# A fourth seven-product pair in the down projection of the first SwiGLU of an encoder trunk

## The chip, the cores and the metric

The kernel runs on one core of one Trainium2 chip. The metric is the device time of one execution in microseconds (us); smaller is better. The engines of the core are TensorE (PE, matrix products), VectorE (DVE), ScalarE (ACT), GpSimd (POOL) and SyncE (SP, which here issues the transfers from HBM). Each works through its own instructions in the order in which the program wrote them, and they wait for one another by semaphores.

## The reference

The model is a trunk of two layers over 256 tokens of width 1024. Each layer adds half a SwiGLU, a mixer (attention) and half a SwiGLU to the residual x; all in float32. The part that the change touches is the SwiGLU ahead of the first mixer:

```python
def swiglu(h, w_gate, w_up, w_down):
    return (jax.nn.silu(h @ w_gate) * (h @ w_up)) @ w_down

    h = rms_norm(x, ffn1_norm[layer])
    x = x + 0.5 * swiglu(h, ffn1_w_gate[layer], ffn1_w_up[layer], ffn1_w_down[layer])
```

`w_gate` and `w_up` are 1024 x 2816, `w_down` is 2816 x 1024. The stages are numbered 0 (SwiGLU), 1 (even mixer), 2, 3 (SwiGLUs), 4 (odd mixer), 5 (SwiGLU).

## The kernel before

**A product.** A float32 operand is kept as two parts, a high one (a copy rounded by ACT, `high_part`) and a low one (the rest, `value - high`, by DVE, `low_part`). A product of a 128 x 128 block of activations with a 128 x 512 block of weights is three matmuls (hi·hi, hi·lo, lo·hi; `mm`, lines 474 to 476), summed in PSUM.

**Weights.** SP loads them in units of 1 MB into one of three `raw` tiles (`load`, line 382). A unit is cut into `Split`s of at most 128 x 1024, each of one or two `Piece`s 512 wide. `supply` makes the high part of the next split, and `low`, a tick later, its low part; when the last split of a unit has its low part, the next unit is loaded. The parts lie in seven places of `wp`, or, where the raw data are sums, in three places of `sum` (`shi`, `slo`). After each product `tick` runs: it adds `rate` pieces to `due`, and supplies a split if as many pieces are due as it has and a place is free (`room`). In stage 0 the rate is 0.6; from the first seven-product pair of the down on it is `DOWN_RATE`, 1.24; after the last such pair `ENDS` sets it to 0.43. Small tasks (silu, glu, transposes, sums) are generators that wait a given number of ticks between their steps. Thus the order of every engine's instructions is fixed by these counts when the program is built.

**The SwiGLU of stage 0** (`ffn`). The width 2816 is done in five chunks of 512 and one of 256 (called mixed, since its gate and up are one operand). The third chunk is itself done with fewer products (`seven_gates`). In each chunk the gate and up products of both halves of the tokens (tt = 0, 1) run, then `silu` (ACT), `glu` (DVE), and `transposed`: the result is turned over (a copy on ACT, L559; a DMA transpose, L561; another copy on ACT, L563) and split into `g_h` and `g_l`, the left operands of the down.

**The down** works through eleven pairs of 128-row blocks of `w_down` in the order of `DOWN[0]`. Pair p3 means blocks 6 and 7, done plainly: 2 blocks x 2 halves of the tokens x 2 halves of the columns are 8 products; s3 means the same by Strassen's scheme in Winograd's form, with 7 products (`seven`). A plain pair needs two splits 1024 wide. A seven-product pair needs four (`strassen`): one 512 wide (b11), then `two_sums` makes `two` on DVE (1024 wide); one 1024 wide of the raw data (b21, b22), then `other_sums` makes two sums of 512 in place in `raw` on DVE (L398); one of `two` (t7, t5) and one of the sums in place (t8, t6). It needs sums of the activations as well (`quarters`, `sums_of`): each half of the tokens is copied by ACT into a `quarters` tile (three tiles in this stage), three sums are made on DVE (lines 716 to 718), and split into `kh` and `kl` (two places). `sums_of` is asked for by `ask`: the first three positions of the order at the start of the mixed chunk, each later one three pairs ahead.

The first products of a seven-product pair go to temporary banks `M`; after the last such pair `combine` adds them to x on DVE (lines 940 to 967). The last two pairs (p10, p9) are held back, so that each quarter of the output can be finished by itself: `add_to_x` (L617) adds it to x on DVE, and a few ticks later `prepare` has PE turn x for the next stage (L530), ACT and DVE split it (`th`, L515; `tl`, L520). The next stage's first weights are `even_w_in`.

Of the kernel before, what the change touches and what calls it, by code (L numbers as in the profile page):

```python
# [33 lines left out]


DOWN = {
# [20 lines left out]
TURN_WAIT = [1, 16]  # L57
SUMS_AHEAD = {0: 3, 2: 3, 3: 3, 5: 4}
QUARTERS = {0: 3, 2: 3, 3: 3, 5: 4}
PLACES = {0: 2, 2: 2, 3: 2, 5: 3}  # L60
SUMS_WAIT = [8, 2]
SILU_WAIT = [3, 4, 2]
# [135 lines left out]
def pairs(stage):  # L198
    return [({"p": "plain", "s": "strassen"}[o[0]], int(o[1:])) for o in DOWN[stage].split()]
# [9 lines left out]
class Trunk:  # L209
# [88 lines left out]
    def plan(self):  # L298
# [56 lines left out]
        def odd():  # L355
# [4 lines left out]
            for g in range(2):  # L360
                for nh in range(2):
                    src = w_out[g * 512 : g * 512 + 512, nh * 512 : nh * 512 + 512].rearrange("(j p) n -> p j n", p=P)
                    yield [(slice(0, P), src)], 4, 512, [2], "narrow"

        yield from ffn("ffn1", 0, 0)
        yield from even()
        yield from ffn("ffn2", 0, 2)
        yield from ffn("ffn1", 1, 3)
        yield from odd()
        yield from ffn("ffn2", 1, 5)  # L370
# [291 lines left out]
    def ffn(self):  # L662
# [4 lines left out]
        down = pairs(self.now.n)  # L667
# [5 lines left out]
        def silu(tt, w, g, s):  # L673
            yield 1
            nc.scalar.activation(s[:, :w], g[:, :w], AF.Silu, scale=self.rstd_of(tt))

        def glu(tt, f0, w, u, s):
            yield 1
            m = self.t([P, 512], "glu", 3)
            nc.vector.scalar_tensor_tensor(m[:, :w], u[:, :w], self.now.r[tt], s[:, :w], op0=ALU.mult, op1=ALU.mult)  # L680
            self.spawn(transposed(tt, f0, w, m), GLU_WAIT)
# [17 lines left out]
        def quarters(tt, f, tb, at):  # L699

            block = lambda i: tb[:, (at + i) * P : (at + i + 1) * P]
            if tt == 0:
                paired[f] = self.t([P, 4, P], "quarters", QUARTERS[self.now.n])
                nc.scalar.activation(paired[f][:, 0:2, :].rearrange("p a b -> p (a b)"), tb[:, at * P : (at + 2) * P], AF.Copy)
# [5 lines left out]
        def sums_of(f):  # L710

            while f not in whole:
                yield 1
            k = paired[f]
            d = k[:, 3:4, :].to_broadcast([P, 2, P])
            nc.vector.tensor_tensor(k[:, 2:4, :], d, k[:, 2:0:-1, :], op=ALU.subtract)
            nc.vector.tensor_tensor(k[:, 1, :], k[:, 2, :], k[:, 1, :], op=ALU.subtract)
            nc.vector.tensor_tensor(k[:, 0, :], k[:, 1, :], k[:, 0, :], op=ALU.add)
            yield SUMS_WAIT[0]
            hi, lo = (self.t([P, 4, P], f"k{p}", PLACES[self.now.n], F32R) for p in "hl")  # L720
            self.high_part(hi, k)
            yield SUMS_WAIT[1]
            self.low_part(lo, k, hi)
            sums[f] = [(hi[:, i, :], lo[:, i, :]) for i in (3, 2, 1, 0)]

        K = []
        sevens = SEVEN[self.now.n]
        most = max(sevens.values())

        def x_sums():  # L730
# [19 lines left out]
            places = [(f"g0_{sum(FF_CHUNKS[:ci]) // P}_", FF_CHUNKS[ci] // P) for ci in range(max(sevens), len(FF_CHUNKS))]  # L750
            places = [(tag, n, 1) for tag, n in places[:2]] + [("k", 4, PLACES[self.now.n])] * 2
            for (tag, n, bufs), k in zip(places, (k0, k1, k2, k3)):
# [3 lines left out]
                self.low_part(lo, k, hi)  # L756
                K.append([(hi[:, q, :], lo[:, q, :]) for q in range(most)])

        def seven_gates(f0, w, pairs7):

            while len(K) < 4:
                self.tick(False)
# [9 lines left out]
            def common():  # L772

                yield 1
                while "m" not in c:
                    yield 1
                w = self.t([P, 512], "silu", SILUS[self.now.n])
                op(w, M["6"], c["m"], op=ALU.add)
                yield 1
                y = self.t([P, 512], "glu", 3)  # L780
                op(y, M["5"], w, op=ALU.subtract)
                yield 1
                nc.vector.scalar_tensor_tensor(w, M["7"], -1.0, w, op0=ALU.mult, op1=ALU.add)
                c["y"], c["w"] = y, w

            def first_gate():
                yield 1
                while "m" not in c:
                    yield 1
                s = self.t([P, 512], "silu", SILUS[self.now.n])  # L790
                op(s, M["00"], c["m"], op=ALU.add)
                yield SILU_WAIT[0]
                nc.scalar.activation(s, s, AF.Silu, scale=self.now.r[0])
                c["s"] = s
# [26 lines left out]
            def product(name, lh, piece, first, last):  # L821
                self.mm(M[name], lh, piece, first, last)
# [5 lines left out]
            for q in range(KD // 2):  # L828
# [19 lines left out]
                if last:  # L848
                    tasks.append(self.start(first_gate()))
                product("01", K[0][j], b22, q == 0, last)  # L850
                product("7", K[3][j], t7, first, last)
                product("5", K[2][j], t5, first, last)
                product("10", h[1][k], t8, q == 0, last)
                product("6", K[1][j], t6, first, last)
            self.start(common())
# [4 lines left out]
        for ci, w in enumerate(FF_CHUNKS):  # L860
            if ci in sevens:
                seven_gates(f0, w, sevens[ci])
                f0 += w // P
                continue
            self.rate = (AHEAD_RATE if ci + 1 in sevens else RATE)[self.now.n]

            tags = ["pj", "s", "s", "pj"] if ci - 1 in sevens else ["s", "s", "pj", "pj"]
            G = self.take(KD)
            S = []
            if self.now.n + ci == 0:  # L870
                both = self.first_gates(G)
            for tt in range(NT):
                g = both[tt] if self.now.n + ci == 0 else self.project(self.ready(tt), G, tags[tt])
                S.append(self.t([P, 512], "silu", SILUS[self.now.n]))
                self.start(silu(tt, w, g, S[tt]))
            U = self.take(KD)
            for tt in range(NT):
                u = self.project(self.now.hT[tt], U, tags[NT + tt])
                tasks.append(self.start(glu(tt, f0, w, u, S[tt])))
            f0 += w // P  # L880

        def ask(i):
            if i < len(down) and down[i][0] == "strassen":
                self.spawn(sums_of(2 * down[i][1]))

        w, V = FF_MIXED, self.take(KD)
        for i in range(SUMS_AHEAD[self.now.n]):
            ask(i)

        for tt in range(NT):  # L890
# [81 lines left out]
        for i, (kind, pair) in enumerate(down[:-HELD]):  # L972
            ask(i + SUMS_AHEAD[self.now.n])
            if kind == "strassen":
                seven(pair, i == order[0], i == order[-1])
                if i == order[-1]:
                    self.start(combine())
                    self.rate, self.due = ENDS[self.now.n]
                continue
            for f in (2 * pair, 2 * pair + 1):  # L980
                W[f] = self.take(2)
                for tt in range(NT):
                    for half in range(2):
                        use(f, tt, slice(half * 512, half * 512 + 512))
# [420 lines left out]
    def after(self, tt, sl, nxt):  # L1405
# [12 lines left out]
        x, gain = self.x[tt], self.last_gain  # L1418
        sq = self.t([P, 4, P], "quarters", QUARTERS[self.now.n]).rearrange("p a b -> p (a b)")
        v = self.two.tile([P, 1], F32, tag="last_v", name=self.name("v"), bufs=6)  # L1420
# [158 lines left out]
```

## Time and profile before

| | us |
|---|---|
| median of 3 runs | 935.45 |
| all runs | 935.42, 935.95, 935.45 |
| the profiled execution, its time | 935.71 |
| its span, first to last instruction | 933.7 |
| PE busy, share of the span | 99% |
| DVE busy, share of the span | 83% |
| ACT busy, share of the span | 72% |
| granted TensorE clock, mean | 0.999 |

A timeline row reads: start in us, duration in us, engine, line, operation, output <- inputs, shape, xcount of merged instructions, and in brackets how long the engine was idle before it and what ended that. PEld is TensorE's load of the stationary operand, SPq is SyncE's queue of transfers. A matmul of 512 columns is drawn 0.39 us long, but the next starts 0.23 us after it, since they are pipelined: starts, not durations, tell PE's pace. Likewise a DVE instruction of 1024 elements is drawn 1.22 us long while its successor starts 1.14 us after it.

In the profiled execution the five chunks and the mixed one of stage 0 end at 127 us, its down lasts to 186 us, and the even mixer follows.

### The profile page before, as it was taken

The numbers are of one execution on the slowest core, as the hardware profiler recorded it, in microseconds if no ns is written. First come the engines' busy times: TensorE is split into PE (matmuls) and PEld (weight loads), VectorE is DVE, ScalarE is ACT, GpSimd is POOL, SyncE is SP. The second block draws the span as 40 slices with busy tenths as digits, with TensorE's granted clock in tenths as the row PEclk, the third lists the DMA queues.
The fourth block names the chain that finished last, engine by engine and source line by source line (L and its number), as shares of the span: only waits on it lengthen the run. The fifth ranks groups of instructions, "written<-read, shape, count | busy, mean of one in ns | idle before, by whom it ended". The sixth has DMA issues, their size and how long they took to land.

```text
span 933.7 us, 12374 instructions
## 1 busy us (share of the span) xinstructions
PE 921.5 (99%) x4405; PEld 754.3 (81%) x4405; DVE 773.4 (83%) x1198; ACT 675.9 (72%) x1084; POOL 92.6 (10%) x152
## 2 busy tenths in 40 slices
PE   9999999999999999999999999999999999999997
PEld 6887888877778888888888888888878888888885
DVE  6799679778868889799878888978867696977898
ACT  7778876467777778885657879657777586778853
POOL 1300000064420000000100000008030000000001
PEclk9999999999999999999999999999999999999999
DMA  8857865644327577757466787566434367588651
GB/s 297 283 172 256 244 213 184 218 142 109 112 92 231 173 237 236 233 191 265 156 193 211 216 278 207 225 210 200 155 99 159 105 204 225 168 265 254 164 212 53
DMA packets 129341, 183.14 MB, mean 196 GB/s; under 512 B 50688, under 2 KB 63744, under 8 KB 129280
## 3 DMA queue, kind: packets, MB, share of 16 engines
q1 hardware_dynamic: 128704, 181.58, 61.8%
q8 instruction: 34, 0.56, 0.2%
q10 hardware_dynamic: 576, 0.79, 0.2%
q14 instruction: 27, 0.22, 0.1%
HBM read 169.76 MB, written 1.05 MB: 183 GB/s over the span
## 4 chain that ended last, share of the span: by engine, by line
PE 88%; DVE 7%; ACT 3%; issue 1%; POOL 0%; POOLq 0%; ACTq 0%; DVEq 0%
PE s L476 13%; PE s L475 13%; PE s L474 12%; PE pj L474 12%; PE pj L475 11%; PE pj L476 11%; DVE lo L485 3%; PE o L474 2%; PE o L476 2%; PE o L475 2%; PE o L1053 2%; PE tp L1130 1%; ACT hi L482 1%; PE tp L530 1%; PE tp L474 1%
## 5 line engine op out<-in xcount | busy, mean ns | idle before, releaser
L485 DVE TENSOR_TENSOR lo<-raw,hi 128x1024 fp32r<-128x1024 f32 (+1 forms) x372 | 377.7, 1034 | 81.8 <-ACT hi L482 80.2
L482 ACT ACTIVATE hi<-raw 128x1024 fp32r<-128x1024 f32 (+1 forms) x372 | 320.1, 892 | 53.9 <-PE s L476 12.6
L474 PE MATMUL s<-hi,th 128*128 128x512 f32 x378 | 148.1, 392 | 0.0
L475 PE MATMUL s<-lo,th 128*128 128x512 f32 x378 | 147.2, 389 | 0.2 <-DVE lo L485 0.2
L476 PE MATMUL s<-hi,tl 128*128 128x512 f32 x378 | 147.2, 390 | 0.0
L474 PE MATMUL pj<-hi,th 128*128 128x512 f32 x366 | 146.2, 399 | 0.0
L475 PE MATMUL pj<-lo,th 128*128 128x512 f32 x366 | 143.2, 391 | 0.6 <-DVE lo L485 0.4
L476 PE MATMUL pj<-hi,tl 128*128 128x512 f32 x366 | 142.8, 390 | 0.0
L475 PEld LDWEIGHTS s<-lo,th 128*128 128x128 f32 x378 | 71.0, 188 | 15.0 <-DVE lo L485 0.5
L476 PEld LDWEIGHTS s<-hi,tl 128*128 128x128 f32 x378 | 70.9, 188 | 14.9
L474 PEld LDWEIGHTS s<-hi,th 128*128 128x128 f32 x378 | 71.0, 188 | 14.5
L475 PEld LDWEIGHTS pj<-lo,th 128*128 128x128 f32 x366 | 68.9, 188 | 15.2 <-DVE lo L485 2.6
L476 PEld LDWEIGHTS pj<-hi,tl 128*128 128x128 f32 x366 | 68.7, 188 | 14.5
L474 PEld LDWEIGHTS pj<-hi,th 128*128 128x128 f32 x366 | 68.8, 188 | 14.0 <-issue 1.0
L494 POOL TENSOR_TENSOR rstd<-var,mhalf 128x1 f32<-128x1 f32 (+2 forms) x16 | 17.1, 1070 | 586.6 <-ACT th L515 309.7
L563 ACT COPY turned<-glu 128x1024 uint16<-128x1024 uint16 (+1 forms) x48 | 60.2, 1253 | 13.2 <-DMA glu<-turned 13.2
L559 ACT COPY turned<-glu 128x1024 uint16<-128x1024 uint16 (+1 forms) x48 | 46.3, 965 | 24.1 <-DVE glu L797 16.3
L482 ACT ACTIVATE shi<-raw 128x1024 fp32r<-128x1024 f32 x28 | 29.6, 1059 | 32.7 <-DVE raw L398 23.0
L474 PE MATMUL s<-hi,g_h 128*128 128x512 f32 (+1 forms) x134 | 52.5, 392 | 0.0
L476 PE MATMUL s<-hi,g_l 128*128 128x512 f32 (+1 forms) x134 | 52.0, 388 | 0.0
L475 PE MATMUL s<-lo,g_h 128*128 128x512 f32 (+1 forms) x134 | 52.0, 388 | 0.0
L482 ACT ACTIVATE shi<-two 128x1024 fp32r<-128x1024 f32 x28 | 29.6, 1058 | 23.8 <-DVE two L398 23.7
(350 smaller groups left out, 1657.3 us busy)
## 6 DMA issues: line engine op xcount, KB each, us to landing
raw<-in_ffn_w_down SPq DMA_DIRECT2D x44, 1024.0 KB, 5.1
raw<-in_ffn_w_up SPq DMA_DIRECT2D x28, 1024.0 KB, 5.1
raw<-in_ffn_w_gate SPq DMA_DIRECT2D x26, 1024.0 KB, 5.3
raw<-in_ffn_w_gate SPq DMA_DIRECT2D x35, 512.0 KB, 4.2
raw<-in_ffn_w_up SPq DMA_DIRECT2D x32, 512.0 KB, 5.2
raw<-in_odd_w_qkv SPq DMA_DIRECT2D x12, 1024.0 KB, 5.2
raw<-in_even_w_in SPq DMA_DIRECT2D x4, 1024.0 KB, 5.1
raw<-in_even_w_out SPq DMA_DIRECT2D x8, 512.0 KB, 5.7
```

The lines of the kernel that those rows point to most:

```text
L474: mm(ps, h, wh, start=first, stop=False)
L475: mm(ps, h, wl, start=False, stop=False)
L476: mm(ps, l, wh, start=False, stop=last)
L482: self.nc.scalar.activation(hi, src, AF.Copy)
L485: self.nc.vector.tensor_tensor(lo, src, hi.bitcast(F32), op=ALU.subtract)
L494: nc.gpsimd.tensor_tensor(r[:, :n], v[:, :n], self.mhalf[:, :n], op=ALU.pow)
L530: nc.tensor.transpose(tb[:, j * P : (j + 1) * P], self.x[tt][:, b * P : (b + 1) * P], self.ident)
L559: self.nc.scalar.copy(planes.rearrange("p (h c) -> p h c", h=2), back.rearrange("p (c h) -> p h c", h=2))
L563: self.nc.scalar.copy(planes.rearrange("p (c h) -> p h c", h=2), back.rearrange("p (h c) -> p h c", h=2))
L1053: self.nc.tensor.matmul(O[64 * s : 64 * s + 64, i * P : i * P + P], v(b0 + i, s, kc), pT[s][:, i, kc, :], start=(kc == 0), stop=(kc == 1),)
L1130: nc.tensor.transpose(tb[:, o : o + P], p[:, i, kc * P : kc * P + P], self.ident)
```

## The change

Pair 1 of the down of stage 0 becomes a seven-product pair, so that there are four (1, 3, 5, 7) and seven plain pairs. Its quarters come from the first chunk. The sums of the first three positions of the order, of which only pair 1 needs any, are asked for at the beginning of the fifth chunk in place of the mixed chunk's. Stages 2, 3 and 5 keep their orders and their time of asking (`None`).

```diff
 DOWN = {
-    0: "p0 p1 p2 s3 p4 s5 p6 s7 p8 p10 p9",
+    0: "p0 s1 p2 s3 p4 s5 p6 s7 p8 p10 p9",
...
+FIRST_SUMS = {0: 4, 2: None, 3: None, 5: None}
...
+        asked = 0
+
+        def ask(i):
+            if i < len(down) and down[i][0] == "strassen":
+                self.spawn(sums_of(2 * down[i][1]))
...
             self.rate = (AHEAD_RATE if ci + 1 in sevens else RATE)[self.now.n]
+            if ci == FIRST_SUMS[self.now.n]:
+                asked = SUMS_AHEAD[self.now.n]
+                for i in range(asked):
+                    ask(i)
...
-        def ask(i):
-            if i < len(down) and down[i][0] == "strassen":
-                self.spawn(sums_of(2 * down[i][1]))
-
         w, V = FF_MIXED, self.take(KD)
-        for i in range(SUMS_AHEAD[self.now.n]):
+        for i in range(asked, SUMS_AHEAD[self.now.n]):
             ask(i)
```

## The prediction

> **What bounds the kernel now.** First the head of the page, then the busy time of one stretch of the down.
>
> ```profile
> span 933.7 us, 12374 instructions
> PE 921.5 (99%) x4405; PEld 754.3 (81%) x4405; DVE 773.4 (83%) x1198; ACT 675.9 (72%) x1084; POOL 92.6 (10%) x152
> ```
>
> ```profile
> 140.00:166.00 26.00, 26.00 (x117) 21.52 (x116) 25.63 (x32) 15.44 (x20) 0.00 (x0) 1.00 0.58 205
> ```
>
> The columns of the stretch are length, PE, PEld, DVE, ACT, POOL, clock, DMA. PE is never idle in the first SwiGLU's down (127 to 186 us). But from 140 to 166 DVE is full too (25.63 of 26), and that stage is where the change puts more DVE work. The DVE rows of one period (s5 with p6 behind it) show the price of each piece, from start to start, with no wait between them:
>
> ```profile
> 142.14 0.42 DVE L716 TENSOR_TENSOR quarters<-quarters 128x256 f32<-128x256 f32 x1
> ...
> 143.13 0.42 DVE L485 TENSOR_TENSOR g_l<-turned,g_h 128x256 fp32r<-128x256 f32 x1
> 143.46 0.69 DVE L485 TENSOR_TENSOR lo<-raw,hi 128x512 fp32r<-128x512 f32 x1
> 144.06 1.22 DVE L398 TENSOR_TENSOR two<-raw 128x1024 f32<-128x1024 f32 x1
> 145.20 1.22 DVE L485 TENSOR_TENSOR lo<-raw,hi 128x1024 fp32r<-128x1024 f32 x1
> 146.34 0.68 DVE L398 TENSOR_TENSOR raw<-two,raw 128x512 f32<-128x512 f32 x1
> 147.06 0.69 DVE L398 TENSOR_TENSOR raw<-raw 128x512 f32<-128x512 f32 x1
> 147.66 1.22 DVE L485 TENSOR_TENSOR slo<-two,shi 128x1024 fp32r<-128x1024 f32 x1
> 148.80 0.42 DVE L485 TENSOR_TENSOR g_l<-turned,g_h 128x256 fp32r<-128x256 f32 x1
> 149.13 0.69 DVE L485 TENSOR_TENSOR kl<-quarters,kh 128x512 fp32r<-128x512 f32 x1
> 149.74 1.22 DVE L485 TENSOR_TENSOR slo<-raw,shi 128x1024 fp32r<-128x1024 f32 x1
> 150.87 2.35 DVE L485 TENSOR_TENSOR lo<-raw,hi 128x1024 fp32r<-128x1024 f32 x2
> ...
> 159.47 0.68 DVE L485 TENSOR_TENSOR kl<-quarters,kh 128x512 fp32r<-128x512 f32 x1
> ```
>
> So: the three sums of quarters 0.99 (142.14 to 143.13), a 512-wide low 0.60, `two` 1.14, a 1024-wide low 1.14, the two sums in place 1.32 (146.34 to 147.66), kl 0.61.
>
> Now the stage's end, as timeline rows of PE, DVE, ACT, SP and PEld:
>
> ```profile
> 127.38 0.39 PE L474 MATMUL o<-hi,g_h 128*128 128x512 f32 x1
> 168.86 0.39 PE L474 MATMUL o<-hi,g_h 128*128 128x512 f32 x1
> 161.21 4.62 DVE L485 TENSOR_TENSOR lo<-raw,hi 128x1024 fp32r<-128x1024 f32 x4
> 163.59 14.92 SPq L382 DMA_DIRECT2D raw<-in_even_w_in  x6
> 171.10 2.20 ACT L482 ACTIVATE hi<-raw 128x512 fp32r<-128x512 f32 x4 [2.36 <-DMA raw<-in_even_w_in]
> 171.77 1.29 DVE L485 TENSOR_TENSOR lo<-raw,hi 128x512 fp32r<-128x512 f32 x2 [2.06 <-ACT hi L482]
> 180.44 0.68 DVE L617 SCALAR_TENSOR_TENSOR x<-o,x 128x512 f32<-128x512 f32 x1
> 181.18 0.42 PEld L530 LDWEIGHTS tp<-mats,x 128*128 128x128 f32 x4 [0.34 <-DVE x L617]
> 184.43 0.60 PE L530 MATMUL tp<-mats,x 128*128 128x128 f32 x4
> ```
>
> This is a chain that ends exactly when PE needs it. The lows from 161.21 are p8's two, then p10's; p8's second ends at about 163.5, frees its raw tile, and SP, which waits for that, issues the mixer's first weights at 163.59. They land at 171.1 (ACT waited 2.36 for them). Their two lows stand in DVE's queue ahead of `combine` (L951 on); DVE then works without a gap from 171.77 to the end of x<-o at 181.12, and the transposes L530, which come next on PE, start at 181.18, after a wait of 0.34 for DVE's x. The matmuls of p8 on follow each other every 0.227 us, so PE was due at these transposes at 181.10. The page's chain names only PE here, since a wait of 0.1 us is all that shows: **two chains arrive together**, PE's products and DVE's lows with the load behind them.
>
> **The change, part by part.** On PE, p0 begins at 127.38 and p8 at 168.86: five plain pairs of 8 products and three of 7, 61 in 41.48 us, 0.68 us each. s1 takes one product away: **-0.68 us**, if PE ends the stage. In the Trainium skill, "TensorE: Matmul & The Clock Gate", section Back-to-back issue gap, an isolated 512-column matmul takes N/2.4 + 2.5, or 216 ns, and a sustained stream 131 ns; here three take 680, 227 each. By the page's two figures the term would be 0.65 or 0.39; the trace decides, and the sign stays.
>
> On DVE, s1 needs a 512-wide low, three 1024-wide lows, `two`, two sums in place, three sums of quarters and kl, where p1 needed two 1024-wide lows. What of it is hidden:
>
> ```profile
> 102.83 3.95 DVE L485 TENSOR_TENSOR lo<-raw,hi 128x1024 fp32r<-128x1024 f32 x3 [2.12 <-ACT hi L482]
> 118.33 1.22 DVE L485 TENSOR_TENSOR lo<-raw,hi 128x1024 fp32r<-128x1024 f32 x1
> 122.65 0.48 DVE L680 SCALAR_TENSOR_TENSOR glu<-s,rstd,silu 128x256 f32<-128x256 f32 x1 [3.10 <-ACT silu L675]
> 124.59 3.95 DVE L485 TENSOR_TENSOR lo<-raw,hi 128x1024 fp32r<-128x1024 f32 x3 [1.46 <-ACT hi L482]
> 129.56 0.69 DVE L485 TENSOR_TENSOR lo<-raw,hi 128x512 fp32r<-128x512 f32 x1 [1.02 <-ACT hi L482]
> 137.52 1.23 DVE L485 TENSOR_TENSOR slo<-raw,shi 128x1024 fp32r<-128x1024 f32 x1 [0.55 <-ACT shi L482]
> ```
>
> The quarters' sums and kl (1.60) go into the fifth chunk, into idle time such as the 2.12 before 102.83: 0. They also release the quarters tile that s7 needs, in time. The 512-wide low and `two` (1.74) stand where p1's first low stood (118.33), before an idle of 3.10: 0; without that cover 0.6. s1's second low replaces p1's second, the first of the three at 124.59: before that wp has no free place (ACT's high parts wait for PE there, as in the row of 126.22 below), so nothing more can move up. **New behind 124.59: two sums in place 1.32 and two lows 2.28, together 3.60 us.** The idle of before between there and 139 that could take it: 1.02, 0.55 and 0.45 within the row at 124.59 (3.95 less two starts of 1.14 and a duration of 1.22), 2.02. From 139.3 to 165.8 DVE has no gap. So the lateness d of p8's lows is at least 3.60 - 2.02 = 1.58 us. It is more if new gaps open, and two do, by ACT's order:
>
> ```profile
> 126.22 1.06 ACT L482 ACTIVATE hi<-raw 128x1024 fp32r<-128x1024 f32 x1 [0.30 <-PE s L476]
> 127.19 0.60 ACT L559 COPY turned<-glu 128x512 uint16<-128x512 uint16 x1
> 127.70 1.35 ACT L563 COPY turned<-glu 128x1024 uint16<-128x1024 uint16 x1
> 129.44 0.62 ACT L482 ACTIVATE g_h<-turned 128x512 fp32r<-128x512 f32 x1
> 129.96 0.46 ACT L675 ACTIVATE silu<-s,rstd 128x256 f32<-128x256 f32 x1
> 133.46 0.62 ACT L559 COPY turned<-glu 128x512 uint16<-128x512 uint16 x1 [0.97 <-DVE g_l L485]
> 133.99 1.37 ACT L563 COPY turned<-glu 128x1024 uint16<-128x1024 uint16 x1
> ```
>
> First gap: the high part of s1's last sums must wait for the sums in place (124.59 + 1.14 + 1.32, about 127.1) and takes p2's place of 126.22; behind it stand L559 (0.51), L563 (1.21), g_h (0.52), the silu (0.5). Each comes a little under 1 us later than before, the glu that needs the silu not before 130.85, while DVE is through with s1 at 129.4 and p2's lows stand behind that glu: 1.45. Second gap: at rate 0.6 the four further pieces of s1 push s3's second split from p0's fourth product to s1's first, behind L559, L563, g_h and kh. L559 waits for g_l as at 133.46, now until 134.2; then 0.53, 1.40, 0.54, 0.52 and the high part's 1.06 give 138.3, when DVE has finished `two` at 136.9: 1.4. So d = 3.60 + 1.45 + 1.4 - 2.02 = **4.4 us**; ends 1.58 (no new gap) and about 5. I take 4.4, since both gaps follow from the written order.
>
> The Trainium skill (the same page, its first table) calls ScalarE's and VectorE's queues strict FIFOs. By that the ready lows can't pass the waiting glu, and d is 4.4; if they could, it would fall towards 1.58. The trace agrees in so far as DVE sat out 3.10 us before the glu of 122.65.
>
> Does d make PE stop earlier? kl of s5 ends at 149.82 + 4.4 = 154.2, needed by s5's third product, now at 154.6; kl of s7 at 164.5 against 164.8; p8's first low at 166.8 against 168.2. All just in time: 0. At the end nothing covers it: p8's raw tile frees d later, the mixer's weights land d later (its neighbour p9 shifts alike), `combine` and x<-o end at 185.5, and PE, there at 180.42 instead of 181.10, waits 5.1 us. The gain of 0.68 is lost in that wait, and the stage ends d later. After it PE is the bound again, with no idle to give back until 200.
>
> Sum: -0.68 (PE) + 5.1 (wait) = **+4.4 us**. The profiled execution took 935.71, span 933.7, 0.26 above the median; the span should come to 938.1, the time to 935.45 + 4.4 = **939.8**. The other edits cost nothing: two copies of quarters more in the first chunk's transposes lie on ACT, which is not on the path; and s1's fifth product, the first on the bank that the last glu frees at about 131.3, comes at 135.5 (127.38 + 12 x 0.68).
>
> **Rivals.** A, as above, 939.8, own range 938.6 to 940.6. B: the order is kinder and DVE uses its idle, d 1.6: 937.0. For it: 2.02 us of gaps are there; against it: ACT's fixed order. C, the other side: PE alone ends the stage, 935.45 - 0.68 = 934.8. Its place is the transposes at 181.18; it decides if x<-o does not come later than 180.4, that is if d is below -0.7. For it: DVE's idle of 2.06 before 171.77; against it: that idle waits for a load which DVE's own lows release, so it moves with them. D: after a wait of 5.1 us PE runs slower for a while. No PE wait of this length is in this trace, so it can't tell; at half pace over the 3.25 us from these transposes to the next (184.43) it would cost that much more: 943. The Trainium skill, the same page, section on the clock gate, says the clock halves after an idle window of about 3.4 us; no run here shows it, the clock of the stretch above being 1.00.
>
> **How the numbers follow.** A 0.58, B 0.16, C 0.12, D 0.09, the rest 0.05 (a later stage gives something back, or kl stops PE too). The range leaves out C and most of D and reaches under B: 936.3 to 941.2. A measurement tells 0.2%, 1.87 us, from no change: slower A, D, a part of B and of the rest, 0.73; same C and most of B, 0.24; faster 0.03.
>
> **What would show it.** Right: x<-o of the first half some 4 us later (near 185), PEld L530 waiting about 5 us for DVE x, the first mixer load issued near 168, no PE wait before. Wrong: no wait at L530 (C), or PE waits at kl or slo in s3 to s7, which would put the price into the alternation itself.

## The result and the profile after

| | us |
|---|---|
| kernel before, median of 4 runs on the same chip | 935.7 (935.42 to 937.47) |
| changed kernel, median of 4 runs | 941.26 (940.74 to 941.88) |
| ratio, 95% interval | 1.0059 (1.0047 to 1.0071) |
| forecast, its range | 939.8 (936.3 to 941.2) |

The change makes the kernel slower by 5.6 us. The sign holds, and so does the chain that the forecast describes; the price that it put on the wait at the end of that chain does not. The size is 1.5 us over it (1.2 as a difference, 5.6 where 4.4 was forecast, since the kernel before came out at 935.7 and not at 935.45), and the median lies 0.06 us above the upper end of the range.

The head of the page of the changed kernel, its profiled execution (941.88 us):

```profile
span 940.1 us, 12375 instructions
PE 922.9 (98%) x4402; PEld 755.3 (80%) x4402; DVE 781.1 (83%) x1207; ACT 678.3 (72%) x1089; POOL 91.2 (10%) x152
```

PE is busy 1.4 us longer although it has fewer products to do, and the span grows by 6.4. PE's waits between 100 and 200 us (engine, line, what it waited for: us in total, times, longest):

```profile
PE tp L531 <- DVE x L618: 4.9, 1, 4.9
```

There is one, at the transposes, where the forecast put it. (In this kernel the lines from the sums on stand one further down than before, those of the SwiGLU's tail one to seven.) Rows of its timeline, DVE, SP, ACT and PE, in order of time:

```profile
98.69 0.42 DVE L717 TENSOR_TENSOR quarters<-quarters 128x256 f32<-128x256 f32 x1
...
104.44 0.69 DVE L486 TENSOR_TENSOR kl<-quarters,kh 128x512 fp32r<-128x512 f32 x1
...
124.56 1.23 DVE L486 TENSOR_TENSOR lo<-raw,hi 128x1024 fp32r<-128x1024 f32 x1 [1.46 <-ACT hi L483]
...
131.03 0.48 DVE L681 SCALAR_TENSOR_TENSOR glu<-s,rstd,silu 128x256 f32<-128x256 f32 x1 [1.57 <-ACT silu L676]
...
138.38 1.23 DVE L486 TENSOR_TENSOR lo<-raw,hi 128x1024 fp32r<-128x1024 f32 x1 [1.27 <-ACT hi L483]
...
163.93 0.68 DVE L486 TENSOR_TENSOR kl<-quarters,kh 128x512 fp32r<-128x512 f32 x1
165.67 4.62 DVE L486 TENSOR_TENSOR lo<-raw,hi 128x1024 fp32r<-128x1024 f32 x4
168.05 24.97 SPq L383 DMA_DIRECT2D raw<-in_even_w_in  x7
175.34 2.20 ACT L483 ACTIVATE hi<-raw 128x512 fp32r<-128x512 f32 x4 [2.05 <-DMA raw<-in_even_w_in]
176.00 1.29 DVE L486 TENSOR_TENSOR lo<-raw,hi 128x512 fp32r<-128x512 f32 x2 [1.75 <-ACT hi L483]
180.16 0.39 PE L477 MATMUL s<-hi,g_l 128*128 128x512 f32 x1
184.67 0.69 DVE L618 SCALAR_TENSOR_TENSOR x<-o,x 128x512 f32<-128x512 f32 x1
185.41 1.11 PE L531 MATMUL tp<-mats,x 128*128 128x128 f32 x4 [4.87 <-DVE x L618]
187.18 0.63 PE L477 MATMUL s<-hi,g_l 128*128 128x512 f32 x1
187.60 0.63 PE L475 MATMUL s<-hi,g_h 128*128 128x512 f32 x1
190.93 0.60 PE L531 MATMUL tp<-mats,x 128*128 128x128 f32 x4
```

The same steps as before, each 4.2 to 4.5 us later: p8's lows 161.21 to 165.67, the mixer's first load 163.59 to 168.05, its lows 171.77 to 176.00, x<-o 180.44 to 184.67. PE is through with the products at 180.39 (the start at 180.16 and 0.227) instead of 181.10, and waits.

The last three rows show what the forecast left out of its sum. Behind the wait PE's matmuls start 0.42 to 0.43 us apart (187.18, 187.60), not 0.227. From these transposes to the next it takes 190.93 - 185.41 = 5.52 us, where it took 184.43 - 181.18 = 3.25 before: **2.27 us more, after the wait has ended.** So the transposes at 190.93 are 6.50 late, 4.23 by x<-o and 2.27 by the pace. The window view of the same kernel gives the granted clock (third column from the end; the first numbers are length and PE's busy time):

```profile
140.00:166.00 26.00, 26.00 (x116) 21.52 (x116) 25.76 (x35) 16.93 (x22) 0.00 (x0) 1.00 0.50 166
...
180.55:183.47 2.92, 0.00 (x0) 0.00 (x0) 2.92 (x6) 0.00 (x0) 0.00 (x0) 1.00 0.05 4
183.48:190.30 6.82, 4.89 (x14) 4.02 (x15) 4.29 (x10) 2.48 (x8) 0.00 (x0) 0.50 0.45 152
190.31:194.00 3.69, 3.69 (x20) 3.06 (x19) 2.77 (x9) 3.34 (x8) 1.75 (x4) 1.00 0.12 7
```

The clock is halved while PE still waits, 2.9 us after its last matmul was drawn to end, and stays at half for 6.8 us, of which 190.30 - 185.41 = 4.9 fall on work. Half of those, 2.4, is about the 2.27 lost.

### The profile page after: what moved, and what is told of

The parts are those of the page before. It is cut to its first block, busy times and chain, and to the rows that moved or that the text cites. A ratio compares the mean times of both kernels' runs of the same rounds, so it can differ in the third digit from the quotient of the medians.

```text
span 940.1 us, 12375 instructions
## 1 busy us (share of the span) xinstructions
PE 922.9 (98%) x4402; PEld 755.3 (80%) x4402; DVE 781.1 (83%) x1207; ACT 678.3 (72%) x1089; POOL 91.2 (10%) x152
## 4 chain that ended last, share of the span: by engine, by line
PE 82%; DVE 10%; ACT 4%; issue 2%; DMA 1%; POOL 0%; POOLq 0%; SPq 0%; ACTq 0%; DVEq 0%
PE s L477 12%; PE s L476 12%; PE s L475 12%; PE pj L475 11%; PE pj L476 11%; PE pj L477 11%; DVE lo L486 4%; PE o L1060 2%; PE o L477 2%; PE o L475 2%; PE o L476 2%; PE tp L1137 1%; ACT hi L483 1%; DVE raw L399 1%; DVE slo L486 1%
```

## The experiments

Three questions: is the price made of x<-o's lateness alone, or also of the clock; is the lateness the sum of DVE's work and the two gaps; and is anything left of the 0.68 us of the product? Each kernel is compared with the kernel before, timed on the same chip; that one's median was 935.76 to 936.35, so differences are taken within a comparison. Line numbers shift by some lines with each edit (the transposes are L531 to L534, x<-o L618 to L621).

**PE kept at work during the wait (e1_busy).** In the changed kernel, 24 matmuls of 384 columns go into the bank of the first transposes, right ahead of them. The transposes overwrite their result, so the output is that of the changed kernel.

```diff
+        if (i, tt, half) == (1, 0, 0):
+            for _ in range(24):
+                nc.tensor.matmul(tb[:, : 3 * P], self.ident16, self.busy, start=True, stop=True)
...
+        self.busy = m16[:, 0 : 3 * P]
```

> The changed kernel with 24 idle matmuls (384 columns, result overwritten) put on PE right ahead of the transposes that wait for x, so that PE is busy in most of that wait and x comes no sooner. Theory (the wait of 4.9 us itself costs 4.2 us, and the lowered clock after it another 2): the wait for DVE x shrinks below 1 us, the matmuls behind it go at 0.227 us each instead of 0.43, granted clock of the span 0.999 instead of 0.995, and the time falls by 1.6 to 2.4 us, to 938.9 to 939.7. Rival (the pace behind the wait is slow for another reason, such as late x or late weights of the mixer): the matmuls stay at 0.43 us and the time at 941.

Measured: 940.02 us (939.64 to 940.21), ratio 1.0042 (1.0027 to 1.0057). Its PE rows:

```profile
180.83 4.08 PE L531 MATMUL tp<-m 128*128 128x384 bf16 x24
185.70 0.66 PE L534 MATMUL tp<-mats,x 128*128 128x128 f32 x4 [0.80 <-DVE x L621]
186.11 0.47 PE L475 MATMUL s<-hi,g_h 128*128 128x512 f32 x1
186.43 0.39 PE L476 MATMUL s<-lo,g_h 128*128 128x512 f32 x1
...
188.97 0.60 PE L534 MATMUL tp<-mats,x 128*128 128x128 f32 x4
```

The transposes come no earlier than in the changed kernel (185.70), but the next ones 3.27 behind them, as in the kernel before. Work of no use, put in a wait that stays, takes the loss from 5.6 (5.9 when the changed kernel was run again, below) to 3.95. So the slow pace belongs to the idle time, not to the transposes or the mixer's operands, and it is 1.6 to 2.0 us of the median; the rest is the lateness of x.

**DVE's lateness alone (e3_two2, e8_two3, e4_two4).** In the kernel before, with its order and its product, the sum `two` of s5 is made three, four or five times (the same values again). That adds 2.28, 3.4 or 4.55 us to DVE in the full stretch and nothing to PE.

```diff
+        self.strassens = getattr(self, "strassens", 0) + 1
+        again = 5 if self.strassens == 5 else 1
...
-            add(two, second[:, 1:2, :].to_broadcast([P, 2, 512]), halves(flat[:, 512:1536]))
+            for _ in range(again):
+                add(two, second[:, 1:2, :].to_broadcast([P, 2, 512]), halves(flat[:, 512:1536]))
```

> The kernel before with the sum two of pair s5 made three times instead of once: 2.28 us of DVE work more. Theory: x<-o 2.3 us later, PE waits 2.5 us at the transposes, its matmuls then keep 0.227 us each (the wait is too short for the clock), granted clock 0.999; time +2.3 us on the kernel before. Rival (the clock falls after any wait above 2 us, so the price per us of lateness is the same as at 4.55 us of extra work, some 1.5 us per us): +3.5.

> The kernel before with the sum two of pair s5 made four times: 3.4 us of DVE work more, between the 2.28 after which PE kept its pace (wait 2.10) and the 4.55 after which it did not (wait 4.73). Theory: PE waits 3.2 us. If the clock falls only after waits above about 3.4 us, the matmuls behind it keep 0.227 us and the time is +3.0 on the kernel before; if it falls from some point between 2.1 and 3.2 on, a part of them takes 0.43 and the time is +4 to +4.8.

> The kernel before, unchanged pairs, with the sum called two of pair s5 made five times instead of once: 4.55 us of DVE work more in the stretch where DVE has no gap. Theory (lateness of DVE's lows is all that counts): x<-o of the first half 4.5 us later, PE waits about 4.9 us at the transposes and nowhere before, then runs slow for 4 to 5 us; time 935.5 + 4.5 + 1.5 to 2.2 = 941.5 to 942.2. Rival (the fourth seven-product pair itself, its order of products or its copies, costs the time): 935.5 to 936.

Measured: 937.62 us, ratio 1.0020 (1.0011 to 1.0029), with two more; 941.11, 1.0055 (1.0040 to 1.0070), with three; 943.31, 1.0078 (1.0062 to 1.0095), with four. DVE and PE rows of the kernel with two more, then of that with four:

```profile
182.29 0.69 DVE L621 SCALAR_TENSOR_TENSOR x<-o,x 128x512 f32<-128x512 f32 x1
183.03 0.66 PE L534 MATMUL tp<-mats,x 128*128 128x128 f32 x4 [2.10 <-DVE x L621]
186.28 0.60 PE L534 MATMUL tp<-mats,x 128*128 128x128 f32 x4
```

```profile
143.95 6.25 DVE L398 TENSOR_TENSOR two<-raw 128x1024 f32<-128x1024 f32 x5
185.57 0.68 DVE L621 SCALAR_TENSOR_TENSOR x<-o,x 128x512 f32<-128x512 f32 x1
186.31 1.12 PE L534 MATMUL tp<-mats,x 128*128 128x128 f32 x4 [4.73 <-DVE x L621]
192.34 0.62 PE L534 MATMUL tp<-mats,x 128*128 128x128 f32 x4
```

Work on DVE alone, in a kernel whose PE does what it did before, brings the whole picture: the wait and, with four more, the half pace (192.34 - 186.31 = 6.03). With two more, x<-o is 1.85 late, the wait is 2.10, the transposes follow at 3.25, and the median is 1.83 above before: lateness alone, no clock. One more, 1.14 us of DVE work, raises the loss from 1.83 to 4.76: by its profile x<-o then comes 2.21 later (184.50), since the last load of the down is waited for longer (DVE stands idle 3.52 us ahead of its lows, 1.61 with two more), and the half clock adds 1.27. Why that load is late was not followed. The price has a step in it. This run was meant to make PE wait 3.2 us; it waited 3.83, so what a wait between 2.10 and 3.67 costs stays open.

**The two gaps (e5_rate, e7_rate_hold, e12_rate_mixed) and the load in the chain (e2_hold, e6_before_hold).** Two edits to the changed kernel. The rate gives the down's 1.24 from the first pair on, not from the first seven-product pair, so that s3's second split is made before DVE asks for it (the second gap). The hold keeps the mixer's pieces back until `combine` is through, so that the mixer's load and its lows no longer stand ahead of the sums.

```diff
+        if self.now.n == 0:
+            self.rate = DOWN_RATE[0]
```

```diff
+        if self.hold and split.narrow:
+            return False
...
+            self.hold = False
...
+                self.hold = self.now.n == 0 and i == order[-1]
```

> The changed kernel with the rate of 1.24 from the beginning of the down instead of from s1 on, so that s3's second split no longer waits for ACT's copies (the gap of 1.27 us on DVE at 137). Theory: most of that gap goes, 0.8 to 1.0 us, p8's last low and x<-o come as much sooner, PE waits 4.0 us instead of 4.9; time 0.9 us below the changed kernel, more if the lowered clock lasts less: 4.0 to 4.7 us above the kernel before of the same chip. Rival (the gaps were harmless, DVE's sum of work alone sets it): within 0.2 us of the changed kernel, 5.6 above.

Measured: 940.62 us, ratio 1.0050 (1.0037 to 1.0064). A DVE and a PE row:

```profile
137.02 1.22 DVE L486 TENSOR_TENSOR lo<-raw,hi 128x1024 fp32r<-128x1024 f32 x1
...
184.22 0.92 PE L531 MATMUL tp<-mats,x 128*128 128x128 f32 x4 [3.67 <-DVE x L618]
```

The low that came at 138.38 after an idle of 1.27 now comes at 137.02 after none, and PE's wait is 1.20 shorter, as x<-o is sooner (183.47): the second gap is one of the terms of the lateness, at its size. The clock is still halved.

> The changed kernel with the mixer's first weights split only after combine, so that combine's eight DVE instructions no longer stand behind lows that wait for a load. Theory (chain of p8's last low, load of even_w_in, its low, combine, x): combine begins at about 174.2 instead of 177.2; four lows still stand ahead of x<-o, which ends at about 182.1 instead of 185.3; PE waits 1.7 us instead of 4.9, its clock stays, time 935.5 + 1.0 = 936.5. Rival (the alternation of s and p pairs itself costs the time): no change, 941.

> The kernel before with the mixer's first weights split only after combine (the edit of e2_hold without the change). Theory: in before PE and x arrive together, so taking DVE's wait for the load out of x's chain can gain at most the 0.1 us that PE waits: 0 to -0.2 us, PE wait for x below 0.1. Rival (the edit itself costs or gains something in the mixer): more than 0.5 us either way.

Measured: with the hold the changed kernel takes 937.14 us (936.5 to 940.58, 10 runs), ratio 1.0019 (1.0009 to 1.0028); the kernel before with the same hold 935.65, ratio 1.0001 (0.9992 to 1.0010). The profiled execution of the first took 938.74; it has a second wait for x, 1.55 us at 451.70, in a later stage, which adds to its time and not to what is read here. Rows of the changed kernel with the hold, and then of the kernel before with it:

```profile
179.46 2.49 DVE L489 TENSOR_TENSOR lo<-raw,hi 128x512 fp32r<-128x512 f32 x4
181.87 0.68 DVE L621 SCALAR_TENSOR_TENSOR x<-o,x 128x512 f32<-128x512 f32 x1
182.60 0.66 PE L534 MATMUL tp<-mats,x 128*128 128x128 f32 x4 [1.70 <-DVE x L621]
```

```profile
177.24 0.69 DVE L620 SCALAR_TENSOR_TENSOR x<-o,x 128x512 f32<-128x512 f32 x1
181.12 0.60 PE L533 MATMUL tp<-mats,x 128*128 128x128 f32 x4
```

In the kernel before the hold brings x<-o 3.2 us forward (180.44 to 177.24) and nothing is gained: PE gets to the transposes at 181.12 as it did. That is the forecast's picture of two chains that arrive together. In the changed kernel the same hold brings x<-o 2.8 forward, and there the time falls. With the load out of the chain the two kernels differ by 181.87 - 177.24 = 4.63 in x<-o, so the lateness is made upstream of that load. The rate edit above and the last kernel below place two parts of it, 1.20 and 1.02, in DVE's own queue.

> The changed kernel with both edits, rate 1.24 from the beginning of the down and the mixer's first weights split after combine. Theory: x<-o ends 0.9 us sooner than in e2_hold, PE waits 0.8 us instead of 1.7, no lowered clock; time -0.7 (the product) + 0.8 = +0.1 to +0.3 us on the kernel before. Rival (what is left in e2_hold is the price of late mixer weights, not of the wait): +1.1 as e2_hold.

Measured with both edits: 935.57 us, ratio 0.9996 (0.9987 to 1.0005). The rows:

```profile
180.38 0.68 DVE L621 SCALAR_TENSOR_TENSOR x<-o,x 128x512 f32<-128x512 f32 x1
181.11 0.66 PE L534 MATMUL tp<-mats,x 128*128 128x128 f32 x4 [0.76 <-DVE x L621]
```

The product saved is there (PE waits 0.76 from the drawn end of its last matmul), but x<-o arrives where it arrived before, so the time is that of the kernel before. What is left is the first gap. A last kernel keeps the hold and gives the rate from the beginning of the mixed chunk, so that p2's two lows stand ahead of the glu that waits for the silu:

```diff
+        if self.now.n == 0:
+            self.rate = DOWN_RATE[0]
         w, V = FF_MIXED, self.take(KD)
```

> The changed kernel with the mixer's pieces held back until the combine is through, as before, and the planner's rate of 1.24 now given from the beginning of the mixed chunk instead of from the beginning of the down, so that the two lows of p2 stand ahead of the up half's last glu, which waits for ACT's silu. Theory (x<-o is late by the sum of DVE's work and gaps in its queue): the gap of 1.57 us ahead of that glu is mostly filled with those lows, x<-o lands 1 to 1.5 us sooner than the 180.38 of the kernel with both edits, the wait of 0.76 us ahead of the first transposes goes, and the median is 0.5 to 0.7 us under the kernel before (about 0.7 is what the product left out saves on PE): ratio 0.9993 to 0.9995. Rival (the gap is only moved, or the lows put first hold up PE in the mixed chunk, which has no cover of this kind before): x<-o as in the kernel with both edits or later, a wait of PE in the mixed chunk, and a median from 0.2 under to 1 us above the kernel before.

Measured: 934.85 us (934.55 to 935.37, 11 runs) beside 935.76 (15 runs), ratio 0.9990 (0.9981 to 0.9999). The rows:

```profile
129.47 2.50 DVE L489 TENSOR_TENSOR lo<-raw,hi 128x1024 fp32r<-128x1024 f32 x2
...
179.36 0.68 DVE L621 SCALAR_TENSOR_TENSOR x<-o,x 128x512 f32<-128x512 f32 x1
180.48 0.60 PE L534 MATMUL tp<-mats,x 128*128 128x128 f32 x4
```

The lows begin at 129.47 without idle, where the changed kernel sat out 1.57 us ahead of the glu; 0.51 of idle comes back at 132.48. x<-o comes 1.02 sooner than with both edits, PE does not wait and starts the transposes 0.70 sooner than in the kernel before (181.18). With the lateness gone, the fourth seven-product pair is worth the product it saves. The median gains 0.9, the interval 0.1 to 1.8. In the kernel before, the hold alone gains nothing; the early rate was not tried there, so that the gain is the product's rests on the 0.70 in the trace.

**Two that cost more than they gave (e2_long, e9_rate_hold2).** In the first the hold lasts until x<-o and x<-pj of the first half are through, and the planner then goes on at a rate of 1.0 with two pieces due. The second has both edits, but nothing due when the hold ends.

```diff
+        if self.hold and sl.start == 512:
+            self.hold, self.rate, self.due = False, 1.0, 2
```

```diff
-            self.hold = False
+            self.hold, self.due = False, 0
```

> The same, but the mixer's weights are split only after both x<-o and x<-pj of the first half of the tokens, then at rate 1. Theory: x<-o ends at 180.0 to 180.4, just when PE comes to the transposes, so no wait above 0.3 us; the product saved is then seen: 935.5 - 0.7 = 934.8, plus up to 1 us if the mixer's first lows, now late, stop PE at 185 to 190. Rival (alternation): 941.

> e7_rate_hold with two of the mixer's lows ahead of x<-o instead of four (nothing is due when they are let go). Theory: x<-o ends 1.2 us sooner, PE's wait of 0.76 goes, and the product saved is seen at last: -0.7 us on the kernel before, the mixer's first lows being in time. Rival (the mixer's lows are now late and stop PE in the mixer, as in e2_long, or the product is worth nothing): 0 to +1.5.

Measured: 938.2 us, ratio 1.0025 (1.0013 to 1.0037), and 958.51, ratio 1.0234 (1.0219 to 1.0249). Neither waits at the transposes. PE's waits behind 180 us, of the first and of the second:

```profile
PE s L1081 <- DVE qTb L489: 3.3, 2, 2.0
PE tp L556 <- DVE kTax L489: 1.1, 1, 1.1
```

```profile
PE pj L479 <- DVE lo L489: 2.3, 5, 0.8
PE s L479 <- DVE lo L489: 2.3, 3, 1.0
```

In the first the lows that were pushed back are done inside the mixer, and PE waits for qTb and kTax behind them (0.6 and 0.7 in the kernel before): the loss has moved on. In the second PE waits for lows again and again. Over the whole execution its waits come to 17.7 us, where the kernel before has 5.5: 12.2 of the 20.9 us by which the span is longer. Where the rest went was not followed. The kernel with both edits differs from it only in what is due when the hold ends, and takes 935.57: a hold must give back what it held.

**The changed kernel once more (e11_after_again).** No edit.

> The changed kernel once more beside the others, so that waits and paces can be compared on one chip. Both theories: 5.2 to 6 us above the kernel before, wait for x 4.9 us, matmuls behind it at 0.43 us for about 4 us.

Measured: 942.28 us (941.05 to 943.66), ratio 1.0060 (1.0043 to 1.0077). Wait and pace come again (4.54, and 5.47 to the next transposes).

That the early sums alone cost nothing was not tried in a kernel of its own; it stands on the trace of the changed kernel alone.

## From the wait to the clock

All waits of PE at these transposes but the one that was filled with matmuls, from the profiled executions, with the time to the next transposes (3.25 before) and the stretch of half clock as the window view shows it:

| kernel | wait | to the next transposes | more | half clock from, to |
|---|---|---|---|---|
| both edits | 0.76 | 3.26 | 0.01 | none |
| hold | 1.70 | 3.25 | 0 | none |
| two more sums | 2.10 | 3.25 | 0 | none |
| rate | 3.67 | 4.85 | 1.60 | 184.48, 187.86 |
| three more sums | 3.83 | 4.52 | 1.27 | 184.58, 187.97 |
| changed kernel again | 4.54 | 5.47 | 2.22 | 183.97, 190.78 |
| four more sums | 4.73 | 6.03 | 2.78 | 185.56, 192.36 |
| changed kernel | 4.87 | 5.52 | 2.27 | 183.48, 190.30 |

Window rows of the rate kernel, and of the changed kernel run again:

```profile
180.55:184.45 3.90, 0.23 (x2) 0.23 (x3) 3.90 (x8) 0.00 (x0) 0.00 (x0) 1.00 0.52 150
184.48:187.86 3.38, 3.38 (x11) 2.77 (x10) 1.53 (x6) 2.47 (x8) 0.00 (x0) 0.50 0.34 131
187.90:192.00 4.10, 4.10 (x21) 3.40 (x20) 3.17 (x10) 3.30 (x8) 1.58 (x4) 1.00 0.08 8
```

```profile
181.46:183.94 2.48, 0.00 (x0) 0.00 (x0) 2.48 (x5) 0.00 (x0) 0.00 (x0) 1.00 0.00 0
183.97:190.78 6.81, 4.79 (x14) 3.92 (x15) 4.38 (x10) 2.47 (x8) 0.00 (x0) 0.50 0.47 154
```

At these transposes the half clock lasts about 3.4 us or about 6.8, nothing between. It begins 2.5 to 4.0 us after PE's last matmul, and in the rate kernel only after PE is at work again. So its length isn't a proportion of the wait. The loss is a little under half of that part of the stretch in which PE has work: (187.86 - 184.48) / 2 = 1.69, where 1.60 was lost; (190.78 - 186.00) / 2 = 2.39, where 2.22 was lost. Windows of 5 us over these executions show no other half clock up to 925 us.

The Trainium skill, "TensorE: Matmul & The Clock Gate", section The HAM clock gate, states a free-running window of 3413 ns, in which activity is watched, and half the rate after at least one idle window. The stretches of 3.4 and 6.8 us agree with one and two such windows, and windows that run free would explain why the onset varies. By that reading an idle window need not be idle throughout: in the changed kernel run again, the clock falls 2.5 us after the last matmul, so if a window of 3.4 us ended there, it held 0.9 us of work.

## Why the prediction was right or wrong

- **What bounds the stage: right.** Two chains arrive together. The hold in the kernel before shows PE's (x<-o 3.2 sooner, nothing gained), the repeated sums show DVE's (1.85 later, 1.83 lost).
- **PE, -0.68: right.** PE ends its products at 180.39, where 180.42 was forecast. The kernel without lateness starts the transposes 0.70 sooner than before.
- **The sums of the activations, 0: right by the trace.** They run at 98.69 and 104.44, and no wait of PE follows.
- **Behind 124.59, 3.60 of new work, 2.02 of old idle, two new gaps: right.** The gaps measure 1.57 and 1.27 (1.45 and 1.4 forecast), the glu starts at 131.03 (not before 130.85), the low at 138.38 (138.3). The lateness of p8's lows is 4.46, that of x<-o 4.23, of 4.4 forecast. Taken out one after the other, the second gap gave back 1.20 of x<-o and the first 1.02.
- **kl just in time, 0: right.** kl of s7 ends at 164.6 (164.5 forecast); PE does not wait for it.
- **The wait, 5.1: right,** 4.87 as drawn, 5.02 from the 180.39 at which PE was through.
- **The price of that wait: wrong, and with it the sum.** The forecast let PE go on at full pace behind the wait (A, 939.8) and made the half pace a rival of its own (D, 943, chance 0.09). But D needs no condition beyond A's own wait of 5.1 us; the two are one case. What the runs show in place of "after it PE is the bound again": waits from 3.67 us on cost another 1.27 to 2.78, waits up to 2.10 nothing. In the profiled execution the terms are 4.23 for x<-o and 2.27 for the clock, together 6.50, beside a span 6.4 longer. The price put on D, 3.25, was too high, 2.27 measured: the clock falls during the wait, so a part of its stretch costs nothing. The other runs of the first comparison, down to 940.74, have no trace; their mean clocks of 0.995 to 0.997 fit one or two stretches, but don't prove them, since the kernel before has 0.997 to 0.999.
- **B, a kinder order: not what happens as written.** The rate edit brings x<-o from 4.23 late to 3.03; only with the hold, which takes the mixer's load out of the chain, is it back at 180.38, in the time of the kernel before. **C, PE alone: no,** until the first gap too is taken out; the last kernel is then 0.9 us under the kernel before, where C had 0.7.

## What to carry to other kernels

Two chains that end together are both to be priced: taking work from the one gains nothing, and what it puts on the other is paid in full, gaps in the order of the queue included. When a forecast contains a new wait of PE of some microseconds, ask in the same sum what PE's clock does behind it, and look at the granted clock in narrow windows around every wait that the trace has. Before such a change is dropped, look for the gaps in the loaded engine's queue: here two of them, 1.57 and 1.27 us, and the load ahead of the sums stood between a loss of 5.6 us and a gain of 0.9.

## What of the hardware was not expected

- The clock is halved in stretches of about 3.4 or 6.8 us, whatever the wait (3.67 to 4.87 us), and stays at 1.00 after waits up to 2.10. Waits between 2.10 and 3.67 were not measured. The 2.10 is no safe limit: at the end of the last kernel, where it costs nothing, the clock falls at 928.4, 2.0 us after PE's last matmul (926.14 and 0.28).
- The stretch can start after the wait has ended: with the rate edit PE is back at 184.22, and the clock falls at about 184.47.
- The order of cost isn't that of the waits: 3.67 us of wait cost 1.60 more, 3.83 us 1.27, since in the latter more of the stretch lay under the wait.
